# A hybrid decoder layer on one core: GpSimd in a fixed order while the attention patterns of one head pair are merged under the next

## The chip, the cores and the metric

The kernel runs on one core of one Trainium2 chip. The core has a matrix engine (TensorE, PE in the profile; PEld is its weight load), a vector engine (VectorE, DVE), a scalar engine (ScalarE, ACT), GpSimd (POOL) and SyncE (SP), which here issues only DMAs. Each engine works through a queue of its own in order, and a DMA is issued by an instruction in one of these queues. The metric is the time on the device of one execution, in microseconds (us).

## The reference

One layer of a causal decoder: a prompt of 2048 tokens and 64 sample tokens, width 1024. One projection feeds two mixers, a dilated softmax attention of 8 heads x 64 (mixer A) and a gated linear attention (mixer B); their outputs go side by side through the output projection `w_o`, and a convolutional feed-forward block follows. The change touches the prompt part of mixer A and the first chunk of the output projection.

```python
PATTERNS = ((128, 1), (512, 4), (2048, 16))       # (window, dilation)
def dilated_prompt(q, k, v, window, dil):
    ...                                           # query t reads keys t - j*dil, j = 0..window/dil
    s = jnp.einsum('brhcie,brhcje->brhcij', qb, kk) * (E ** -0.5)
    s = jnp.where(mask, s, NEG)
    lse = jax.nn.logsumexp(s, axis=-1)
    p = jnp.exp(s - lse[..., None])
    o = jnp.einsum('brhcij,brhcje->brhcie', p, vv)
    ...
    return o, lse
```

Every head is computed in three patterns. The three outputs of a head and position are then averaged with weights in proportion to their softmax denominators, exp(lse) of each over the sum of the three: this is the merge.

## The kernel before

**How the attention is cut.** `attention` (L986 on) works through four pairs of heads (`pr` 0 to 3; the two heads of a pair fill 128 columns). A pair has three patterns (`pat` 0 to 2, dilation 1, 4 and 16) of four groups `g`, twelve groups in all, counted here 0 to 11; the groups of patterns 0 and 1 are cut into two units each, those of pattern 2 are one unit, so there are 20 units per pair. For a unit, `AtUnit.qk_` issues the score matmuls (`pas`, L1787), a masked row minimum on VectorE (L1792) and the exponential on ScalarE (L1796). `drain` runs two and three units behind: the transposes of the probabilities (L1813, copied to `apt`), and the product with V into `pao` (L1830), of which VectorE copies the finished group to the block `aop` of that pattern (L63). `aop` has five buffers; a pair fills three, one for each pattern.

**Operands.** Patterns 1 and 2 read queries with a stride; GpSimd gathers them two groups ahead (`at_gather`, two copies `aqg` per group, L1118). SyncE loads Q and K of the next pair in pieces (`at_load`, L1073, a generator advanced once per group) and blocks of V (`at_loadv`, four DMAs each, L1085).

**The merge.** When the last unit of a pair is through, `at_merge` is made as a generator for that pair. Its first step aligns the three patterns' minima and sums by matmuls (`pam`), computes the three weights per head and position in small steps on [128 x 32] pieces (L1151 to L1166), transposes them, copies them to `awt` and stores them in DRAM (`d_awd`, L1184). A weight block is then loaded by GpSimd's queue as two DMAs, each a row of weights that all 64 partitions of a head receive (`awb`, two buffers, L1173). Four blocks `cb` follow: on GpSimd, three products of `aop` with the weights (L1211) and two sums (L1215, L1217) into `amo`, which is stored to `mixa` (L1219). `attention` advances the generator once per group of patterns 0 and 1 of the next pair. For pair 3 there is no next pair: its weights reach the columns through TensorE transposes (`pab`, L1208), the products are VectorE's (L1209), and its stores are on SyncE.

**What sets the order.** The Python order of the calls, as issued, gives a scheduler its program, and for GpSimd the scheduler may move instructions against each other; TensorE's attention instructions are chained in program order by `AtUnit.line`.

**Behind the attention.** `wo_pre` loads and splits the first operands of the output projection (`WORD`, four of mixer B, k = 4 to 7) during pair 3, `wo_x` the others: k = 0 to 3 are read back from `mixa`. A split makes the pieces `xh` and `xl` on ScalarE or VectorE (L71 is its subtraction). The matmuls are in `wo` (`pbo`, L1405).

## Time and profile before

| what | us |
|---|---|
| median of three timed runs | 2848.71 |
| lowest and highest of them | 2837.03, 2849.65 |
| the profiled execution, its own time | 2844.27 |
| the profiled execution, its span | 2842.5 |
| TensorE busy, whole span | 2682.9 (94%) |
| VectorE busy | 1841.9 (65%) |
| ScalarE busy | 1268.1 (45%) |
| GpSimd busy | 602.3 (21%) |

The profile is one execution as the hardware recorded it. Its page gives each engine's busy share, the span in 40 slices of 71 us with one digit per engine (tenths busy) and the TensorE clock that was granted, and groups of instructions. A row of a group or of the timeline reads: line and engine, operation, output <- inputs by the program's names (numbers cut off), shape, count; `[4.50 <-DMA d_mixa<-amo]` means that the engine was idle for 4.50 us before it and that this transfer ended the idle time. In a timeline the row begins with its start and its duration, in us. In the table of windows a row gives the start and end, the length, then for PE, PEld, DVE, ACT, POOL the busy time with the number of instructions, then the granted clock, the DMA share and GB/s.

### The profile page before, as it was taken

How to read it: one execution, taken by the hardware profiler on the slowest of the kernel's cores; microseconds unless marked ns; L12 is line 12 of the kernel's file. 1: busy time of each engine (PE TensorE's matmuls, PEld its weight loads, DVE VectorE, ACT ScalarE, POOL GpSimd, SP SyncE). 2: the span in 40 equal slices, each digit the busy share in tenths (PEclk: the TensorE clock that was granted, in tenths of full speed). 3: DMA queues.
4: the chain of work that ended last, by engine and by line, in shares of the span. 5: the costliest groups of instructions: out<-in, count | busy, mean ns of one | idle time of the engine just before them, and what ended most of it. 6: DMA issues, size and time to landing. Idle time of an engine off the chain costs nothing. (4 is left out here: it accounts for less than half of the span.)

```text
span 2842.5 us, 58662 instructions
## 1 busy us (share of the span) xinstructions
PE 2682.9 (94%) x22255; PEld 2529.1 (89%) x22255; DVE 1841.9 (65%) x4557; ACT 1268.1 (45%) x2958; POOL 602.3 (21%) x751
## 2 busy tenths in 40 slices
PE   7999999999988967998899999999999999999997
PEld 6788899788877856998899999899999999999997
DVE  7667654443356746466889988676567766666666
ACT  6535433333267855344455545443334433443332
POOL 3424242443324557003110002000020000200001
PEclk9999999999989989999999999999999999999998
DMA  8755445898888745267488668787588875876654
GB/s 296 256 176 183 166 146 180 299 329 328 288 176 172 180 113 126 92 207 284 173 284 297 234 224 306 277 289 265 199 313 285 294 264 190 323 256 216 221 191 146
DMA packets 285657, 657.09 MB, mean 231 GB/s; under 512 B 31856, under 2 KB 82672, under 8 KB 283328
## 3 DMA queue, kind: packets, MB, share of 16 engines
q1 hardware_dynamic: 254880, 576.50, 60.5%
q0 software_dynamic: 13408, 44.99, 5.1%
q10 hardware_dynamic: 17088, 31.86, 3.0%
q8 instruction: 175, 2.87, 0.4%
q14 instruction: 106, 0.87, 0.1%
HBM read 509.29 MB, written 143.94 MB: 230 GB/s over the span
## 5 line engine op out<-in xcount | busy, mean ns | idle before, releaser
L68 ACT ACTIVATE ws<-wr 128x512 fp32r<-128x512 f32 (+1 forms) x482 | 293.0, 616 | 434.3 <-PE pfe L1559 135.6
L90 PE MATMUL pfd<-hh,ws 128*128 128x264 f32 x2816 | 475.5, 285 | 8.7 <-ACT ws L68 4.4
L90 PEld LDWEIGHTS pfd<-hh,ws 128*128 128x128 f32 x2816 | 399.5, 188 | 11.9 <-ACT ws L68 5.8
L71 DVE TENSOR_TENSOR ws<-wr,ws 128x512 fp32r<-128x512 f32 (+1 forms) x482 | 319.4, 668 | 140.0 <-ACT ws L68 136.4
L90 PE MATMUL pfd<-hl,ws 128*128 128x264 f32 x1408 | 303.0, 284 | 1.2 <-DVE hl L71 1.2
L1559 PE MATMUL pfa<-xh,ws 128*128 128x264 f32 x1496 | 293.2, 287 | 5.5 <-ACT ws L68 3.2
L1559 PE MATMUL pfe<-xh,ws 128*128 128x264 f32 x1496 | 289.9, 286 | 4.0 <-DMA ws<-d_wst 2.5
L1559 PE MATMUL pfd<-xh,ws 128*128 128x264 f32 x1408 | 289.2, 285 | 0.3 <-DVE gt L1546 0.2
L1559 PEld LDWEIGHTS pfa<-xh,ws 128*128 128x128 f32 x1496 | 237.4, 190 | 7.5 <-ACT ws L68 3.9
L1559 PEld LDWEIGHTS pfe<-xh,ws 128*128 128x128 f32 x1496 | 237.4, 190 | 4.6 <-DMA ws<-d_wst 2.7
L396 PE MATMUL pv<-wh,xh 128*128 128x256 f32 (+1 forms) x816 | 234.2, 287 | 1.1 <-DVE th L693 1.1
L1559 PEld LDWEIGHTS pfd<-xh,ws 128*128 128x128 f32 x1408 | 231.9, 189 | 0.7 <-DVE gt L1546 0.4
L396 PE MATMUL pv<-wl,xh 128*128 128x256 f32 (+1 forms) x816 | 231.8, 284 | 0.0
L396 PE MATMUL pv<-wh,xl 128*128 128x256 f32 (+1 forms) x816 | 231.0, 283 | 0.0
L90 PEld LDWEIGHTS pfd<-hl,ws 128*128 128x128 f32 x1408 | 225.3, 188 | 1.6 <-DVE hl L71 1.6
L1796 ACT ACTIVATE ass<-ass,aml 128x256 f32<-128x256 f32 (+1 forms) x384 | 173.6, 454 | 112.4 <-DVE aml L1792 86.8
L1508 POOL DMA_DIRECT2D xl<-d_xst x52 | 28.6, 551 | 892.4 <-PE pfe L1559 856.5
L1559 PE MATMUL pfd<-xl,ws 128*128 128x264 f32 x704 | 200.9, 285 | 0.0
L90 PE MATMUL pq<-xh,wh 128*128 128x512 f32 (+2 forms) x480 | 174.4, 371 | 10.2 <-ACT xh L234 7.8
L1559 PE MATMUL pfa<-xl,ws 128*128 128x264 f32 x616 | 176.7, 287 | 0.7 <-DMA xl<-d_xst 0.7
L1559 PE MATMUL pfe<-xl,ws 128*128 128x264 f32 x616 | 175.2, 285 | 0.0
L90 PE MATMUL pq<-xl,wh 128*128 128x512 f32 (+2 forms) x480 | 173.7, 363 | 0.0
(335 smaller groups left out, 6609.4 us busy)
## 6 DMA issues: line engine op xcount, KB each, us to landing
ws<-d_wst SPq DMA_DIRECT2D x248, 512.0 KB
wr<-in_wu SPq DMA_DIRECT2D x114, 512.0 KB
d_wst<-ws SPq DMA_DIRECT2D x88, 512.0 KB
wr<-in_wd SPq DMA_DIRECT2D x160, 256.0 KB
wr<-in_wt SPq DMA_DIRECT2D x60, 512.0 KB
wh<-d_wbs SPq DMA_DIRECT2D x35, 512.0 KB
wl<-d_wbs SPq DMA_DIRECT2D x35, 512.0 KB
skp<-in_ckt SPq DMA_DIRECT2D x16, 1024.0 KB
```

Source lines behind the costliest of these rows:

```text
L68: h = nc.scalar.activation(hi, src, AF.Copy)
L71: return h, (nc.gpsimd if lo_eng == "p" else nc.vector).tensor_tensor(lo, src, hi.bitcast(F32), op=ALU.subtract)
L90: mm = nc.tensor.matmul(o, ww[:, k, :], xx[:, s0:s0 + n], start=(k == order[0] and i == 0), stop=(k == order[-1] and i == 2))
L396: mm = nc.tensor.matmul(ps[:m, :256], x[:, t0:t0 + m], w[:, k % 4, :], start=(k == 0 and i == 0), stop=(k == KT - 1 and i == 2))
L1508: self.nc.gpsimd.dma_start(t.bitcast(F32), xo[i, z])
L1559: self.lastmm = nc.tensor.matmul(bank[:, :H], w[:, ww, k, :], xx, start=new and k == 0 and j == 0, stop=k == 3 and j == 2, skip_group_chec ...
L1796: ex = nc.scalar.activation(ssb[:, sc:sc + nk], ssb[:, sc:sc + nk], AF.Exp, bias=self.ml[:, idx, h:h + 1], scale=-1.0, accum_out=self.ml[: ...
```

## The change

- A new `line` chains GpSimd's work of the attention in the order in which the program issues it: gathers, the store of the weights, their loads, products, sums and stores. The merge of pair 3 isn't chained, apart from its stores.
- The merge generator is advanced in every group of the next pair (before: groups 0 to 7), and a block takes two groups: products of patterns 0 and 1 and their sum (now into the block of pattern 1) in one, the product of pattern 2, the second sum and the store in the other. Two more stops lie around the store of the weights.
- The loads of the next pair's Q and K are advanced in groups 5 to 10 (before: 0 to 7).
- The small steps of the merge are VectorE's for pairs 0 to 2 and GpSimd's for pair 3 (before: the other way round).
- The weights lie in another order in DRAM, so that a block is read as one run of 1536 elements per partition (before: twelve runs of 128).
- `amo` has two buffers, and pair 3 takes `amo` from a ring of six (`ass`); `apt` has four buffers, not five; pair 3's stores are GpSimd's.
- The eight DMAs of the first two V blocks are issued by GpSimd, not by SyncE.
- `wo_pre` prepares three operands (k = 4, 5, 6), `wo_x` five (k = 7 and 0 to 3); the piece of k = 3 that chunk 0 needs is split straight from pair 3's `amo`, and not read back.

```diff
-    AB = dict(... pt=5 ... ms='ppps' ...)
+    AB = dict(... pt=4 ... ms='pppp' ...)
...
-            p.tile([128, 512], F32, name=self.n("amo"), tag="amo", bufs=1)
+            for _ in range(2):
+                p.tile([128, 512], F32, name=self.n("amo"), tag="amo", bufs=2)
...
-                        if pend is not None and pat < 2:
+                        if pend is not None:
                             next(pend, None)
-                        if pat < 2:
+                        if 5 <= 4 * pat + g < 11:
                             self.qk0 = next(nxt, self.qk0)
...
     def at_loadv(self, i):
-        nc = self.nc
+        nc, e = self.nc, self.nc.gpsimd if i < 2 else self.nc.sync
...
+    def line(self, ins):
+        if self.atpo is not None:
+            self.after(ins, self.atpo)
+        self.atpo = ins
+        return ins
...
-            self.nc.gpsimd.tensor_copy(t, src)
+            self.line(self.nc.gpsimd.tensor_copy(t, src))
...
-        em = nc.vector if pr == 3 or not AB["em"] else nc.gpsimd
+        em, line = (nc.gpsimd, lambda x: x) if pr == 3 else (nc.vector, self.line)
...
-                    nc.gpsimd.dma_start(W[64 * h:64 * h + 64],
-                                      bass.AP(tensor=wd.tensor, offset=wd.offset + 128 * h + 256 * cb,
-                                              ap=[[0, 64], [4096, 3], [1024, 4], [1, 128]]))
+                    line(nc.gpsimd.dma_start(W[64 * h:64 * h + 64],
+                                           bass.AP(tensor=wd.tensor, offset=wd.offset + 1536 * (2 * cb + h),
+                                                   ap=[[0, 64], [512, 3], [128, 4], [1, 128]])))
...
-            nc.gpsimd.dma_start(wd, wt)
+            yield
+            line(nc.gpsimd.dma_start(wd, wt))
+            yield
             nxt = weights(0)
...
             for i in range(3):
+                if i == 2 and not last:
+                    line(nc.gpsimd.tensor_tensor(OP[1][:, :, sl], OP[1][:, :, sl], OP[0][:, :, sl], op=ALU.add))
+                    yield
...
-                    (nc.gpsimd if j % 12 < AB["mp"] else nc.vector).tensor_tensor(
-                        OP[i][:, :, sl], OP[i][:, :, sl], W[:, i], op=ALU.mult)
+                    line(nc.gpsimd.tensor_tensor(OP[i][:, :, sl], OP[i][:, :, sl], W[:, i], op=ALU.mult))
...
-            e.tensor_tensor(OP[0][:, :, sl], OP[0][:, :, sl], OP[1][:, :, sl], op=ALU.add)
...
+            if last:
+                mo = self.aq[1].tile([128, 512], F32, name=self.n("amo"), tag="ass", bufs=AB["s"])
+            else:
+                mo = p.tile([128, 512], F32, name=self.n("amo"), tag="amo", bufs=2)
...
+            le(e.tensor_tensor(mo.rearrange("p (m r) -> p r m", r=4),
+                               OP[1][:, :, sl], OP[2][:, :, sl], op=ALU.add))
+            line(nc.gpsimd.dma_start(self.a["mixa"][:, pr, 512 * cb:512 * cb + 512], mo))
+            if last and cb < 2:
+                if cb == 0:
+                    self.xnext[3] = self.hl()
+                o, m = ((0, 512), (512, 2 * H - 512))[cb]
+                self.split(*(t[:, o:o + m] for t in self.xnext[3]), mo[:, :m], "v")
...
-        for k in self.WORD[:4]:
+        for k in self.WORD[:3]:
...
-        for k in self.WORD[0 if c else 4:]:
+        for k in self.WORD if c else self.WORD[3:7]:
```

What the change does to the order shows on three engines. The first place is GpSimd's queue in pair 1, where the merge of pair 0 begins. Of before, the rows from the store of the weights on (`awb` are weight blocks, `aop` the three patterns' outputs, `aqg` gathered queries; a number is the program's own):

```order
L1184 DMA d_awd_73<-awt_1767_10587 96x128
L1173 DMA awb_1768_10590<-d_awd_73 64x12x128 x2
L1173 DMA awb_1790_10691<-d_awd_73 64x12x128 x2
L1211 TENSOR_TENSOR aop_1519_9386<-aop_1519_9386,awb_1768_10590 128x4x128
L1211 TENSOR_TENSOR aop_1592_9725<-aop_1592_9725,awb_1768_10590 128x4x128
L1211 TENSOR_TENSOR aop_1676_10101<-aop_1676_10101,awb_1768_10590 128x4x128
L1211 TENSOR_TENSOR aop_1519_9386<-aop_1519_9386,awb_1790_10691 128x4x128
L1211 TENSOR_TENSOR aop_1592_9725<-aop_1592_9725,awb_1790_10691 128x4x128
L1211 TENSOR_TENSOR aop_1676_10101<-aop_1676_10101,awb_1790_10691 128x4x128
L1215 TENSOR_TENSOR aop_1519_9386<-aop_1519_9386,aop_1592_9725 128x4x128
L1118 COPY aqg_1820_10821<-aqs_1590_9721 128x512
L1118 COPY aqg_1842_10927<-aqs_1529_9444 128x512
```

And the same place of the changed kernel:

```order
L1195 DMA d_awd_73<-awt_1767_10585 96x128
L1126 COPY aqg_1789_10688<-aqs_1630_9901 128x512
L1126 COPY aqg_1790_10690<-aqs_1686_10160 128x512
L1183 DMA awb_1808_10778<-d_awd_73 64x1536 x2
L1126 COPY aqg_1812_10788<-aqs_1630_9901 128x512
L1126 COPY aqg_1813_10790<-aqs_1686_10160 128x512
L1183 DMA awb_1831_10878<-d_awd_73 64x1536 x2
L1225 TENSOR_TENSOR aop_1520_9387<-aop_1520_9387,awb_1808_10778 128x4x128
L1225 TENSOR_TENSOR aop_1589_9714<-aop_1589_9714,awb_1808_10778 128x4x128
L1210 TENSOR_TENSOR aop_1589_9714<-aop_1589_9714,aop_1520_9387 128x4x128
L1126 COPY aqg_1833_10889<-aqs_1630_9901 128x512
L1126 COPY aqg_1834_10891<-aqs_1686_10160 128x512
```

Before, both weight blocks are loaded and six products and a sum stand together ahead of the next gathers; now a pair of gathers stands between the store, the first load, the second load and the second half step, and the first sum follows its two products.

The second place is SyncE's queue at the start of the attention (`aqs`, `akh`, `akl` are pieces of Q and of the two parts of K, `av` blocks of V). Before:

```order
L1073 DMA aqs_1488_9209<-d_qh0_57 64x512
L1073 DMA akh_1494_9246<-d_kh0_65 64x512 x2
L1085 DMA av_1502_9349<-out_o_vp 128x1x128 x4
L1085 DMA av_1503_9354<-out_o_vp 128x1x128 x4
L1073 DMA akl_1497_9277<-d_kl0_69 64x512 x2
L1085 DMA av_1520_9387<-out_o_vp 128x1x128 x4
L1073 DMA aqs_1479_9116<-d_qh0_57 64x2x512
```

And now:

```order
L1074 DMA aqs_1488_9209<-d_qh0_57 64x512
L1074 DMA akh_1494_9246<-d_kh0_65 64x512 x2
L1074 DMA akl_1497_9277<-d_kl0_69 64x512 x2
L1086 DMA av_1521_9388<-out_o_vp 128x1x128 x4
L1074 DMA aqs_1479_9116<-d_qh0_57 64x2x512
```

The eight DMAs of two V blocks are gone from between `akh` and `akl`; they stand in GpSimd's queue.

The third place is VectorE's queue at the end of pair 3's merge and the start of the output projection (`pab` are transposed weights, `xl` is the second piece of a split operand, `br` a raw operand). Before:

```order
L1209 TENSOR_TENSOR aop_2369_13432<-aop_2369_13432,pab_2446_13872 128x4x128
L1215 TENSOR_TENSOR aop_2176_12575<-aop_2176_12575,aop_2269_13012 128x4x128
L1217 TENSOR_TENSOR amo_2438_13831<-aop_2176_12575,aop_2369_13432 128x4x128
L1217 TENSOR_TENSOR amo_2443_13857<-aop_2176_12575,aop_2369_13432 128x4x128
L71 TENSOR_TENSOR xl_2452_13899<-br_2453_13900,xh_2451_13898 128x528
L71 TENSOR_TENSOR xl_2455_13905<-br_2456_13906,xh_2454_13904 128x528
```

And now:

```order
L71 TENSOR_TENSOR xl_2431_13800<-amo_2429_13795,xh_2430_13799 128x512
L1233 TENSOR_TENSOR aop_2266_12993<-aop_2177_12576,aop_2266_12993 128x4x128
L1223 TENSOR_TENSOR aop_2266_12993<-aop_2266_12993,pab_2444_13865 128x4x128
L1223 TENSOR_TENSOR aop_2177_12576<-aop_2177_12576,pab_2443_13858 128x4x128
L71 TENSOR_TENSOR xl_2431_13800<-amo_2436_13825,xh_2430_13799 128x16
L1223 TENSOR_TENSOR aop_2364_13410<-aop_2364_13410,pab_2445_13872 128x4x128
L1235 TENSOR_TENSOR amo_2441_13853<-aop_2266_12993,aop_2364_13410 128x4x128
L1233 TENSOR_TENSOR aop_2266_12993<-aop_2177_12576,aop_2266_12993 128x4x128
L1235 TENSOR_TENSOR amo_2446_13879<-aop_2266_12993,aop_2364_13410 128x4x128
L1353 MEMSET halo_16438 128x44
L71 TENSOR_TENSOR xl_2452_13900<-br_2453_13901,xh_2451_13899 128x528
L71 TENSOR_TENSOR xl_2455_13906<-br_2456_13907,xh_2454_13905 128x528
```

Two splits straight from `amo` (512 and 16 columns) now stand among the merge's steps, the two last sums write to buffers of the larger ring, and the splits of the operands that are read from DRAM still come behind both sums.

More of the change, by code (lines that the diff above doesn't have):

```diff
@@ L1134, in at_merge @@
         else:
-            tm = p.tile([128, 512], F32, name=self.n("atm"), tag="amo", bufs=1)
+            tm = p.tile([128, 512], F32, name=self.n("atm"), tag="amo", bufs=2)
         nc.vector.tensor_tensor(tm[:, :256].rearrange("p (o b x) -> p o b x", o=16, b=4),
@@ L1180, in at_merge @@
             nc.tensor.transpose(pt[:96, :128], awf, self.ident)
-            wt = p.tile([128, 512], F32, name=self.n("awt"), tag="amo", bufs=1)[:96, :128]
+            wt = p.tile([128, 512], F32, name=self.n("awt"), tag="amo", bufs=2)[:96, :128]
             self.evac(wt, pt[:96, :128], "v")
             wd = self.a["awd"][pr]
-            nc.gpsimd.dma_start(wd, wt)
+            yield
+            line(nc.gpsimd.dma_start(wd, wt))
+            yield
             nxt = weights(0)
@@ L1195, in at_merge @@
                 W, nxt = nxt, weights(cb + 1) if cb < 3 else None
-            mo = p.tile([128, 512], F32, name=self.n("amo"), tag="amo", bufs=1)
             for i in range(3):
+                if i == 2 and not last:
+                    line(nc.gpsimd.tensor_tensor(OP[1][:, :, sl], OP[1][:, :, sl], OP[0][:, :, sl], op=ALU.add))
+                    yield
                 if last:
```

34 lines of the change are left out of this document (17 added, 17 removed).

## The prediction

> **What bounds the kernel now.** I read the page first: TensorE (PE) is busy nearly everywhere and falls at one place only, the slices from 780 to 1140 us, which are the prompt attention. Its granted clock falls there too.
>
> ```profile
> span 2842.5 us, 58662 instructions
> PE   7999999999988967998899999999999999999997
> PEclk9999999999989989999999999999999999999998
> ```
>
> The profiled execution took 2844.27 us, that is its span and 1.8 us around it; the three timed runs have a median of 2848.71, so the sum below, made against 2844.27, may lie 4 us below a median. Next I read TensorE's timeline for the first score matmul of each pair (one row per pair), and of three pattern-16 groups (842.69, 853.83 and 988.85).
>
> ```profile
> 779.83 0.22 PE L1787 MATMUL pas<-akh,aqs 128*128 128x128 f32 x1
> 842.69 0.33 PE L1787 MATMUL pas<-akh,aqg 128*128 128x128 f32 x1
> 853.83 0.33 PE L1787 MATMUL pas<-akh,aqg 128*128 128x128 f32 x1
> 857.69 0.33 PE L1787 MATMUL pas<-akh,aqs 128*128 128x128 f32 x1
> 939.78 0.33 PE L1787 MATMUL pas<-akh,aqs 128*128 128x128 f32 x1
> 988.85 0.33 PE L1787 MATMUL pas<-akh,aqg 128*128 128x128 f32 x1
> 1008.23 0.33 PE L1787 MATMUL pas<-akh,aqs 128*128 128x128 f32 x1
> 1103.24 0.33 PE L1787 MATMUL pas<-akh,aqg 128*128 128x128 f32 x1
> ```
>
> The pairs take 77.9, 82.1, 68.5 and, up to the last group at 1103.24, 95.0 us. Undisturbed they would take this: pair 2 needs 988.85 - 939.78 = 49.1 us for its first eight groups, in which nothing waits, and pair 0 needs 857.69 - 842.69 = 15.0 us for four groups of pattern 16, of which the last starts after 11.1. So an **undisturbed pair is 64.1 us**, its group 11 starting at 60.2. Who waits in 800 to 1160 us, from the view of waits on TensorE, its three longest lines:
>
> ```profile
> PE pao L1830 <- DVE aop L63: 22.8, 1, 22.8
> PE pas L1787 <- POOL aqg L1118: 21.8, 4, 10.7
> PE pbo L1405 <- DVE xl L71: 7.6, 1, 7.6
> ```
>
> Two of them are GpSimd (POOL). 21.8 us are gathers that stand behind a merge. The 22.8 us, in pair 3, are a VectorE (DVE) copy that waits until the merge of pair 1 has finished with its first block; the rows show that merge waiting for its weights and adding only at 1033:
>
> ```profile
> 1028.99 3.70 POOL L1211 TENSOR_TENSOR aop<-aop,awb 128x512 f32<-128x512 f32 x3 [3.19 <-DMA awb<-d_awd]
> 1033.27 2.49 POOL L1215 TENSOR_TENSOR aop<-aop,aop 128x512 f32<-128x512 f32 x2
> 1036.91 1.34 PE L1830 MATMUL pao<-apt,av 128*64 128x128 f32 x10 [22.78 <-DVE aop L63]
> 999.57 0.33 PE L1787 MATMUL pas<-akh,aqg 128*128 128x128 f32 x1 [2.33 <-POOL aqg L1118]
> ```
>
> The last row prices what follows a short wait: pair 2 took 68.45 us, 64.1 and 2.3 of waiting, so **2.0 us** went to the slower clock behind it.
>
> **Pairs 1 to 3: the new GpSimd order.** It has the same 16 gathers, 12 products and 8 additions per merge, but each merge is spread over eleven groups, and a gather now stands in a fixed place between half steps. I price that queue from these rows (products, gathers; then issues with KB each and median time to landing).
>
> ```profile
> L1118 POOL CAST aqg<-aqs 128x512 fp32r<-128x512 f32 x60 | 64.3, 1100 | 39.9 <-PE pas L1787 38.5 <-issue 1.5
> L1211 POOL TENSOR_TENSOR aop<-aop,awb 128x512 f32<-128x512 f32 x36 | 44.6, 1269 | 34.3 <-DMA awb<-d_awd 34.3
> L1173 POOL DMA_DIRECT2D awb<-d_awd x24 | 18.0, 756 | 9.8 <-DMA d_awd<-awt 8.0 <-issue 1.7
> awb<-d_awd POOLq DMA_DIRECT2D x24, 384.0 KB, 10.9
> d_mixa<-amo POOLq DMA_DIRECT2D x12, 256.0 KB, 3.8
> d_awd<-awt POOLq DMA_DIRECT2D x3, 48.0 KB, 4.3
> 876.37 0.56 POOL L1184 DMA_DIRECT2D d_awd<-awt  x1 [2.61 <-DVE awt L63]
> 884.26 2.99 POOL L1173 DMA_DIRECT2D awb<-d_awd  x4 [7.34 <-DMA d_awd<-awt]
> 897.10 7.36 POOL L1211 TENSOR_TENSOR aop<-aop,awb 128x512 f32<-128x512 f32 x6 [9.84 <-DMA awb<-d_awd]
> ```
>
> In pair 1 the weights are stored at 876.37, 18.7 us after the pair began. The copy ahead of the store now stands one unit (2.9 us) later in VectorE's order, so 21.6. Then come the store (0.6), its landing La, the issue of the first weight block (1.5), its landing Lw, and the first product starts at 23.7 + La + Lw. From there to the first gather of group 11 the fixed order holds three leading half steps (3 x 1.27 = 3.8 each), two trailing ones (2 x 1.27 and a store of 0.6: 3.1 each), two weight issues (1.5 each) and nine gathers (1.1 each): 11.4 + 6.2 + 3.0 + 9.9 = 30.5 us. The gather is then ready at 54.2 + La + Lw, and TensorE wants it at 60.2, so it comes **late by La + Lw - 6.0**. The groups of pattern 16 last 3.7 us, while two gathers and half a step take 6: that is why the wait gathers there.
>
> La: 7.3 us where the loads of the next pair's Q and K run beside it (the wait in the row at 884.26), 4.3 in the median; I take 5.5 for pairs 1 and 2 and 4.3 for pair 3, which loads no next pair. Lw is unknown, since no weight block is loaded in runs of 6 KB before. The upper bound is today's: 12.8 from issue (884.26) to first use (897.10), less the 1.5 of issuing, 11.3. The nearest row from below is the store of `mixa` from the same queue, 256 KB in unbroken rows, 3.8. A block is 768 KB; at the 222 GB/s of a busy stretch (row below) that is 3.5 us, and 2 for the rest: I take Lw = 5.5. Pairs 1 and 2 are late by 5.0, pair 3 by 3.8; with 2.0 for the clock that makes 64.1 + 7.0 = **71 us** for each of pairs 1 and 2 (gains of 11.1, and a loss of 2.5), and 60.2 + 5.8 = **66.0** for pair 3 up to its group 11, a gain of 29.0. Bounds: nothing late gives 64.1 and 60.2; Lw = 11.3 and La = 7.3 give 78.7 twice and, with La = 4.3, 71.8.
>
> The Trainium skill prices this load by itself: "DMA: Bandwidth & Descriptors", section "Anatomy of one DMA", fits 2.0 us and bytes / 436e3 for a DMA from GpSimd, so 3.8 us as an estimate for a block of 768 KB. The row of 10.9 us for half of it does not agree with that for today's loads; by that price the sum would be 5 us lower.
>
> The 22.8 us go with the same order: the block of the merged pair that the next copy needs is free after the last leading half step, 7 us behind the last gather, at about 72, and TensorE needs the copy for its third product of pattern 16, two units into the next pair, at about 76. The margin is 4 us; without it that much would come back.
>
> Beside other work, at nothing: the small merge steps, now on VectorE, are 12 of about 0.2 us per merge (row below), 2.4 us under pairs in which VectorE is busy for 50.6 of 68; uncovered they cost 7 in all. The transposed blocks fall from 5 to 4, but TensorE's fixed order finishes the product of unit n-4 before it transposes unit n-2; uncovered, that is a product of 1.0 us per unit. `amo` gets a second buffer, which only removes waits. In SyncE's order the next pair's loads keep their place behind the buffers they wait for; uncovered, a pair would start with the 1.8 us of waiting for a piece that the row at 805.57 below shows.
>
> ```profile
> L1155 DVE TENSOR_TENSOR aaw<-aw,amm 128x32 f32<-128x32 f32 x2 | 0.4, 188 | 0.0
> 940.00:1008.00 68.00, 65.47 (x657) 58.17 (x658) 50.56 (x231) 56.02 (x217) 32.97 (x42) 0.97 0.73 163
> ```
>
> **Pair 0.** SyncE issues eight loads of V ahead of a K piece that TensorE wants. They move to GpSimd's queue, so the pieces behind them are issued up to 7.5 us sooner.
>
> ```profile
> 777.47 7.51 SPq L1085 DMA_DIRECT2D av<-out_o_vp  x8
> 780.00:790.00 10.00, 4.91 (x28) 4.36 (x28) 4.32 (x24) 4.99 (x21) 0.54 (x1) 0.77 0.57 158
> 790.00:800.00 10.00, 5.03 (x36) 4.23 (x34) 3.17 (x15) 4.55 (x16) 1.09 (x1) 0.84 1.01 222
> 805.57 0.55 PE L1787 MATMUL pas<-akl,aqs 128*128 128x256 f32 x1 [1.75 <-DMA akl<-d_kl]
> ```
>
> But the same bytes must land before 805.57, and only the ten microseconds with a DMA share of 0.57 have room: 4.3 us at most, 0 at least. I take 2.9: pair 0 becomes **75.0**. The eight issues delay GpSimd's last store of V by about 4.5 us; its columns belong to pairs 2 and 3, and the first gather starts only at 794.
>
> **The end.** From the last group to the output projection it takes 1142.69 - 1103.24 = 39.45 us. TensorE waits there for operand pieces (`xl`) that VectorE writes behind the last two sums of pair 3:
>
> ```profile
> 1137.41 1.06 DVE L1217 TENSOR_TENSOR amo<-aop,aop 128x512 f32<-128x512 f32 x1 [4.50 <-DMA d_mixa<-amo]
> 1141.00 1.10 DVE L1217 TENSOR_TENSOR amo<-aop,aop 128x512 f32<-128x512 f32 x1 [2.53 <-DMA d_mixa<-amo]
> 1141.93 2.55 DVE L71 TENSOR_TENSOR xl<-br,xh 128x528 fp32r<-128x528 f32 x4
> 1142.69 0.81 PE L1405 MATMUL pbo<-xl,wh 128*128 128x264 f32 x2 [7.63 <-DVE xl L71]
> ```
>
> Both sums wait for a store out of the one `amo` buffer: 4.50 + 2.53 = 7.0 us. Pair 3 now takes its buffers from a ring of six, so these go. Added are two splits straight from the sums (a split is 2.55 / 4 = 0.6 at 528 columns; 512 and 16 columns make 0.8 together). One block of matmuls (k = 7) that ran under the wait now stands behind it: 0.7. That is 39.45 - 7.0 + 0.8 + 0.7 = **34.0**. Late next is VectorE itself, with its products of pair 3. Bounds: the whole 7.63 gone, or 3 if the splits and the block cost twice what I put down and the small steps of pair 3, now on GpSimd (12 at 246 ns and not at 188: +0.7), stand on the path.
>
> **Sum.** Before: 77.9 + 82.1 + 68.45 + 95.0 + 39.45 = 362.9. After: 75.0 + 71 + 71 + 66.0 + 34.0 = 317.0. The gain of 45.9 makes 2844.27 - 45.9 = **2798 us**.
>
> **Rivals.**
> *All is hidden.* The weights land as fast as the stores (3.8 us), the gathers of pattern 16 are in time, and the pairs take 64.1, 64.1 and 60.2: with 75.0 and 34.0 that is 297.4, so **2779**. For it: the row of 3.8 us from the same queue. Against it: the load is three times that store (768 KB a block), and the queue has only 60.2 - 54.2 = 6.0 us for La + Lw. Chance 0.18.
>
> *The loads are no faster.* Lw stays 11.3, La 7.3: 78.7, 78.7, 71.8, 75.0 and 34.0 make 338.2, so **2820**. For it: what fills the DMA engines in a merge is the same bytes in both kernels, and the share was 0.73 to 1.01 in the rows above. Against it: 768 KB in 11.3 us is 68 GB/s where other stretches reach 222. Chance 0.17. The Trainium skill speaks for this rival: "DMA: Bandwidth & Descriptors", section "Specifications", sets the smallest transfer for line rate at 512 B, which today's runs have already. The trace does not bear that out alone, as the 384 KB of 512 B runs take 10.9 us against 3.8 for 256 KB in rows; which of size and run length does it, no row says.
>
> *Slower: the gathers are held behind the weights.* In the fixed order a late block stops every gather behind it, and TensorE with them, where today a scheduler's order put gathers as they came. The price is La + Lw - 6.0 in each of three merges. It eats the whole gain when the three pairs lose another 45.9 / 3 = 15.3 each, that is from La + Lw = 26.3 on, against 11.0 in my sum. The slowest landing of half a block is below:
>
> ```profile
> DMA to landing us min/median/max: 7.0/10.9/16.6
> ```
>
> 16.6 + 7.3 = 23.9, still under 26.3. A merge of eleven groups must also be done before its `aop` blocks are wanted again, and the margin of 4 us above could fall with it; both together give about 2860. Chance 0.04.
>
> *No change.* The order doesn't do what it says: the groups of pattern 16 wait as long in sum as the two longest waits of TensorE now, 22.8 + 21.8 = 44.6, and only the clock and the end move: 2830 to 2858. Chance 0.08.
>
> **How the numbers follow.** Forecast 2798 with 0.53, the rivals 0.18, 0.17, 0.04 and 0.08. Half a per cent, 14 us, is about what a measurement of this kernel can tell from no change. The forecast and the first two rivals are all faster by more: 0.88; the same 0.08, slower 0.04. The range goes from the first rival less 5 (pair 0 at 73.6 and the end at 31.8 would be 3.6 less), 2774, to the second plus 4 (pair 0 at 77.9, the end 1 us longer), 2824; it leaves out the last two rivals.
>
> **What would show it.** Right: no wait of TensorE for the copy of `aop` (22.8 now); its waits for `aqg` in short pieces in groups 8 to 11 of pairs 1 to 3, 3 to 6 us a pair, with `awb` as what GpSimd waits for; `awb` landing in 4 to 7 us; the first score rows of the pairs some 75, 71 and 71 us apart; sums of pair 3 without a wait for `d_mixa`. The second rival shows in a median landing of `awb` near 11, the first in no wait for `aqg` at all. Pair 0 is wrong if the first wait for `akl` stays. The forecast fails if a new long wait stands on TensorE: for `apt`, of which there are four, for a piece of Q or K at a pair's start, or for weights stuck behind the V loads on GpSimd's queue.

## The result and the profile after

The changed kernel takes 2799.83 us (median of four runs, 2796.51 to 2802.07), the kernel before 2849.18 (2837.03 to 2849.88): a ratio of **0.9836, 95% interval 0.9808 to 0.9864**. The profiled execution took 2799.56 us, 44.7 less than the one before. In the page TensorE's share rises with its busy time unchanged, and the five slices of the attention stand at 8, 9, 9, 9 and 8 tenths (8, 8, 9, 6 and 7 before):

```profile
span 2797.8 us, 58627 instructions
PE 2685.3 (96%) x22255; PEld 2532.2 (91%) x22255; DVE 1844.2 (66%) x4580; ACT 1268.5 (45%) x2959; POOL 595.0 (21%) x741
PE   7999999999989998998999998999999999999997
PEclk9999999999999999998999999999999999999998
```

TensorE's timeline, first score matmul of each pair and of the last group (line 1809 now):

```profile
781.37 0.22 PE L1809 MATMUL pas<-akh,aqs 128*128 128x128 f32 x1
855.13 0.33 PE L1809 MATMUL pas<-akh,aqs 128*128 128x128 f32 x1
931.24 0.33 PE L1809 MATMUL pas<-akh,aqs 128*128 128x128 f32 x1
1008.70 0.33 PE L1809 MATMUL pas<-akh,aqs 128*128 128x128 f32 x1
1074.05 0.33 PE L1809 MATMUL pas<-akh,aqg 128*128 128x128 f32 x1 [2.78 <-POOL aqg L1126]
```

The landmark of the end, the matmul that waited for `xl`, has no wait any more. I use the last matmul of the output projection in its place, from the view by line; its last start stands ahead of the semicolon. Before:

```profile
L1405 PE MATMUL pbo<-xh,wl x512: 279/284/422, 1132.2 to 1336.6; 128*128 128x264 f32 x171
```

And after:

```profile
L1427 PE MATMUL pbo<-xh,wl x512: 278/284/423, 1100.6 to 1297.0; 128*128 128x264 f32 x171
```

So the 44.7 us go where this table says (the end: last group to last output matmul, 1336.6 - 1103.24 = 233.4 before and 1297.0 - 1074.05 = 222.9 after):

| stretch | before | after | change | forecast |
|---|---|---|---|---|
| pair 0 | 77.9 | 73.8 | -4.1 | -2.9 |
| pair 1 | 82.1 | 76.1 | -6.0 | -11.1 |
| pair 2 | 68.5 | 77.5 | +9.0 | +2.5 |
| pair 3 to its last group | 95.0 | 65.4 | -29.7 | -29.0 |
| the end | 233.4 | 222.9 | -10.4 | -5.5 |
| all before and behind these | | | -3.6 | 0 |

The last line I don't put down to the change, which touches nothing there: what follows the output projection took 1497.0 to 1507.3 us in the profiles of the fourteen kernels here, and 1505.9 and 1500.8 in these two. Without it, -41.2 was measured where -45.9 was forecast. The end varies too, from 220.7 to 226.9 us in the ten kernels here whose operations at the end are the changed kernel's.

The large waits of before (22.8 for the copy of `aop`, 21.8 for gathers) are gone. Of TensorE's waits from 780 to 1110 us these are the three longest; the first was forecast by no step:

```profile
PE pao L1852 <- DMA av<-out_o_vp: 10.4, 4, 3.9
PE pas L1809 <- POOL aqg L1126: 6.8, 5, 2.8
PE pas L1809 <- DMA akh<-d_kh: 4.0, 1, 4.0
```

The forecast priced pairs 1 to 3 by one quantity, the sum La + Lw of two landings. GpSimd's timeline gives it: the store of the weights, then the first product of the merge, less 0.5 for the store and 1.5 for the issue. First pair 1, then pair 2, then pair 3:

```profile
877.54 0.53 POOL L1195 DMA_DIRECT2D d_awd<-awt  x1 [27.72 <-PE pao L1852]
895.24 2.48 POOL L1225 TENSOR_TENSOR aop<-aop,awb 128x512 f32<-128x512 f32 x2 [8.54 <-DMA awb<-d_awd]
954.51 0.54 POOL L1195 DMA_DIRECT2D d_awd<-awt  x1 [15.29 <-DVE awt L63]
973.13 2.52 POOL L1225 TENSOR_TENSOR aop<-aop,awb 128x512 f32<-128x512 f32 x2 [4.78 <-DMA awb<-d_awd]
1031.73 0.53 POOL L1195 DMA_DIRECT2D d_awd<-awt  x1 [14.52 <-DVE awt L63]
1042.73 2.98 POOL L1225 TENSOR_TENSOR aop<-aop,awb 128x512 f32<-128x512 f32 x2 [2.11 <-DMA awb<-d_awd]
```

895.24 - 877.54 - 2.0 = 15.7, and likewise 16.6 and 9.0, where 11.0, 11.0 and 9.8 were put down. The first issue of weights lies between the two (pairs 1, 2 and 3):

```profile
882.50 1.05 POOL L1183 DMA_DIRECT2D awb<-d_awd  x2 [2.21 <-DMA d_awd<-awt]
962.81 1.04 POOL L1183 DMA_DIRECT2D awb<-d_awd  x2 [5.57 <-DMA d_awd<-awt]
1034.44 1.04 POOL L1183 DMA_DIRECT2D awb<-d_awd  x2
```

From its end to the first product it is 11.7, 9.3 and 7.2 us, where Lw was 5.5; from the end of the store to the issue it is 4.4, 7.8 and at most 2.2, where La was 5.5, 5.5 and 4.3. (Gathers run under both; in pairs 2 and 3 one of them waits for TensorE, and the product still waits for the weights behind it.) Into the forecast's own rule (late by La + Lw - 6.0, 2.0 for the clock) the sums give 75.8, 76.7 and 65.2 us; measured were 76.1, 77.5 and 65.4. That made the question for the experiments: is it this landing that sets the pairs, or V, for which TensorE waits by the list, and what makes the landing long?

Times below are medians of device time. The changed kernel's four runs span 2796.5 to 2802.1, so a few us can't be told from 2800 by times alone; the stretches of the trace can be read finer. The kernel before, timed again beside each group of runs, has medians from 2844.7 to 2849.2.

### The profile page after: what moved, and what is told of

The parts are those of the page before. It is cut to its first block, busy times and chain, and to the rows that moved or that the text cites. A ratio compares the mean times of both kernels' runs of the same rounds, so it can differ in the third digit from the quotient of the medians.

```text
span 2797.8 us, 58627 instructions
## 1 busy us (share of the span) xinstructions
PE 2685.3 (96%) x22255; PEld 2532.2 (91%) x22255; DVE 1844.2 (66%) x4580; ACT 1268.5 (45%) x2959; POOL 595.0 (21%) x741
## 4 chain that ended last, share of the span: by engine, by line
PE 76%; DMA 9%; DVE 7%; POOL 3%; ACT 2%; issue 2%; SPq 1%; ACTq 0%; DVEq 0%; POOLq 0%
PE pfd L90 17%; PE pv L396 9%; PE pfe L1581 8%; PE pfa L1581 8%; PE pfd L1581 8%; PE pq L90 7%; PE pbo L1427 5%; PE pfb L1581 4%; PE pas L1809 2%; PE pao L1852 1%; DMA ws<-d_wst 1%; PE pat L1835 1%; DMA raw<-in_xp 1%; DVE ws L71 1%; POOL aop L1225 1%
## 5 line engine op out<-in xcount | busy, mean ns | idle before, releaser
L90 PEld LDWEIGHTS pfd<-hh,ws 128*128 128x128 f32 x2816 | 401.7, 189 | 10.9 <-ACT ws L68 5.3
L90 PEld LDWEIGHTS pfd<-hl,ws 128*128 128x128 f32 x1408 | 226.9, 189 | 1.7 <-DVE hl L71 1.7
L1609 DVE TENSOR_TENSOR acc<-acc,pfd 128x264 f32<-128x264 f32 x304 | 116.9, 427 | 91.3 <-PE pfd L90 91.0
```

What stands on the lines that cost most here:

```text
L90: mm = nc.tensor.matmul(o, ww[:, k, :], xx[:, s0:s0 + n], start=(k == order[0] and i == 0), stop=(k == order[-1] and i == 2))
L1609: nc.vector.tensor_tensor(acc[m][:, s0:s0 + n], acc[m][:, s0:s0 + n], pz, op=ALU.add)
```

## The experiments

### The two halves of the new order

**No chain.** GpSimd's queue is left to the scheduler again; steps, groups and loads stay as changed.

```diff
     def line(self, ins):
-        if self.atpo is not None:
-            self.after(ins, self.atpo)
-        self.atpo = ins
         return ins
```

> The changed kernel without the chain on GpSimd: the half steps, the groups and the loads stay, but the scheduler is free to order GpSimd's queue. If the fixed order carries the gain of pairs 1 to 3 (45 us of it), gathers stand behind whole blocks again: long waits of TensorE for gathered queries, 2825 to 2845 us. If the half steps over eleven groups do it by themselves, the time stays within 5 us of 2800.

2812.03 us (2808.83 to 2814.61; ratio 0.9867, interval 0.9843 to 0.9891), between the two expectations. Pairs 1 to 3 take 85.2, 72.9 and 73.8 us, 12.9 more in sum than with the chain, and the waits of before come back in small (from TensorE's waits, 780 to 1110 us):

```profile
PE pas L1806 <- POOL aqg L1123: 20.0, 7, 8.0
PE pao L1849 <- DVE aop L63: 6.8, 2, 4.9
```

So the chain is worth some 12 us, about half of the 26.7 us by which pairs 1 to 3 are shorter than before (245.6 then, 218.9 now), and not the gain.

**Whole steps.** The chain stays, but a block's second half is no longer put off to the next group.

```diff
                 if i == 2 and not last:
                     line(nc.gpsimd.tensor_tensor(OP[1][:, :, sl], OP[1][:, :, sl], OP[0][:, :, sl], op=ALU.add))
-                    yield
```

> The half steps undone: a block (three products, two sums, store) stands whole between the gathers of two groups, in the same fixed order; merges then end by group 7 of the next pair. Theory (queue): the gathers of groups 6 and 7 stand behind whole blocks and a first load of 16 us: a pair waits 6 to 10 us more there than with half steps but catches up behind group 8: pairs 1 to 3 lose 0 to 8 us each, 2805 to 2820 us. Rival: the half steps are worth most of what the fixed order is not, some 30 us: 2830 us.

2846.74 us; against the kernel before a ratio of 1.0007 (0.9989 to 1.0026): **the whole gain is gone**, more than either theory said. The first product comes as early as ever (40.3 us after the start of pair 1), but TensorE waits at every block. Its timeline in pair 1:

```profile
905.97 0.47 PE L1808 MATMUL pas<-akh,aqg 128*128 128x128 f32 x1 [5.28 <-POOL aqg L1126]
916.39 0.33 PE L1808 MATMUL pas<-akh,aqg 128*128 128x128 f32 x1 [1.79 <-POOL aqg L1126]
926.74 0.47 PE L1808 MATMUL pas<-akh,aqg 128*128 128x128 f32 x1 [6.55 <-POOL aqg L1126]
936.03 0.48 PE L1808 MATMUL pas<-akh,aqg 128*128 128x128 f32 x1 [2.83 <-POOL aqg L1126]
```

The idle times sum to 16.5 us in this pair, and the pair takes 89.8 us. Pair 0 and the end keep their gains in this run (73.9 and 224.4 us), so pairs 1 to 3, at 257.2 us in sum, are even worse than before the change (245.6), and some 38 us worse than with half steps. The half steps make the fixed order work. I had expected the lost time to be caught up behind the merge; the rows show why it isn't: each wait is followed by the next block.

### Is it V or the weights?

**No Q and K.** Left out: the loads of Q and K for pairs 2 and 3, which compute with pair 1's.

```diff
-                nxt = self.at_load(pr + 1) if pr < 3 else iter(())
+                nxt = self.at_load(pr + 1) if pr < 1 else iter(())
```

> Left out: the loads of Q and K for pairs 2 and 3 (these pairs compute with pair 1's), 6.3 MB less in the windows of pairs 1 and 2 each. Theory (weights): pairs 1 and 2 (76.1 and 77.5 us now) are long because the first weight block lands late beside these loads; store and block then take 9 to 10 us in sum as in pair 3, and a pair takes 64.1 + 3.5 + 2 = 69 to 70 us: 2784 to 2788 us, with short waits for gathers left and none for V. Rival (V): what sets the pairs is V arriving late; no wait is left and a pair takes 64 to 66: 2774 to 2780 us.

Pairs 1 and 2 take 69.0 and 71.2 us, about as the theory of the weights says (69 to 70); 2793.54 us (2789.23 to 2799.12), 5.5 above its range. First products come 33.4 and 34.3 us after their pair's start, La + Lw is 9.0 and 8.9, and what waits is the gathers:

```profile
PE pas L1809 <- POOL aqg L1126: 9.3, 6, 2.8
```

The run takes traffic from beside V as well: it shows that the weights still hold the pairs when V is in time, not that V held nothing.

**No V.** Left out: the loads of V for pairs 1 to 3, which compute with pair 0's last block.

```diff
     def at_loadv(self, i):
+        if i >= 12:
+            self.vq += self.vq[-4:]
+            return
```

> Left out: the loads of V for pairs 1 to 3 (they compute with pair 0's last block), so no product can wait for V. Theory (weights): the waits for V (10.4 us) turn into waits for gathers, since these were due at the same time; pairs 1 and 2 keep 70 to 77 us, less only by what the first weight block lands sooner: 2788 to 2800 us. Rival (V): the waits for V go and nothing takes their place, pairs 1 and 2 take 64 to 67 us: 2774 to 2782 us.

2780.99 us (2776.43 to 2782.2), by its time what the rival says. But the trace shows pairs 1 and 2 at 71.5 and 66.1, with gathers waited for, as the theory says, and with La + Lw at 10.0 and 6.7. By time this run spoke for V, by its parts for the weights: taking V away also takes traffic from beside the weights, so it can't tell the two apart. That is done by three runs made for other ends (below), whose code in pair 1 is the changed kernel's, and whose loads differ only in pair 0 or at the end. TensorE's waits in pair 1, of the changed kernel:

```profile
PE pao L1852 <- DMA av<-out_o_vp: 7.0, 3, 3.9
```

Of the run in which `mixa` is read back:

```profile
PE pas L1804 <- POOL aqg L1126: 8.4, 4, 3.7
```

And of that with the first V loads on SyncE (in the third, with one buffer at the end, it is 6.4 us for gathers and none for V):

```profile
PE pas L1809 <- POOL aqg L1126: 8.8, 4, 4.2
```

In one execution TensorE waits for V and never for a gather, in three others for gathers and never for V, and the pair takes 76.1 us in the first and 79.0, 79.4 and 76.1 in these: both come at about the same time, the list names the one that was a little later, and without a wait for V the pair is no shorter. The run with the small steps on GpSimd (below) shows the other side: there the first product of pair 1 comes 2.8 us sooner than in the changed kernel, TensorE waits for V alone, and the pair still takes 75.7 us:

```profile
PE pao L1852 <- DMA av<-out_o_vp: 7.3, 3, 5.4
```

So either of the two, left alone, holds pair 1 at about 76 us. What the runs with this order of GpSimd share is a rule, counted not from La + Lw but from the pair's start, so that it also takes pairs whose store is late: a pair lasts as long as its first product takes to come, and 36.4 us more (30.5 of queue, 3.9 for the last group, 2.0 for the clock); pair 3 to its last group, 32.5 more. The queue came out as forecast: from the first product to the end of the last gather, one gather more than in the 30.5, pair 1 shows 30.7 to 31.8 us in the ten kernels that keep this order. A part of their thirty pairs:

| run, pair | first product after | by the rule | measured |
|---|---|---|---|
| changed, 1 | 40.1 | 76.5 | 76.1 |
| changed, 2 | 41.9 | 78.3 | 77.5 |
| changed, 3 | 34.0 | 66.5 | 65.4 |
| no Q and K, 1 | 33.4 | 69.8 | 69.0 |
| no V, 2 | 31.9 | 68.3 | 66.1 |
| short runs, 2 | 42.5 | 78.9 | 80.0 |
| V on SyncE, 1 | 42.8 | 79.2 | 79.4 |
| Q and K later, 2 | 46.2 | 82.6 | 83.2 |
| small steps on GpSimd, 1 | 37.4 | 73.8 | 75.7 |

The rule misses by 2.2 us at most. In the last row, 1.9 over it, V holds the pair: its last gather was done 7.5 us before the pair's end, in pair 1 of the others 4.3 to 6.1.

### What makes the landing long?

**Short runs.** The weights lie in DRAM as before the change, and a block is read in runs of 512 bytes.

```diff
-        at = lambda i: cap(aw, 4 * i, [[1, 4], [24, 4], [12, 2]])
+        at = lambda i: cap(aw, 32 * i, [[8, 4], [2, 4], [1, 2]])
...
-                                           bass.AP(tensor=wd.tensor, offset=wd.offset + 1536 * (2 * cb + h),
-                                                   ap=[[0, 64], [512, 3], [128, 4], [1, 128]])))
+                                           bass.AP(tensor=wd.tensor, offset=wd.offset + 128 * h + 256 * cb,
+                                                   ap=[[0, 64], [4096, 3], [1024, 4], [1, 128]])))
...
-                    src = cap(aw, 24 * cb + 4 * i, [[1, 4], [12, 2], [0, 64]])
+                    src = cap(aw, i * 32 + 2 * cb, [[8, 4], [1, 2], [0, 64]])
```

> The weights lie as before the change, so a block is loaded in runs of 512 bytes and not of 6 KB. Theory: the run length is worth what the first block's landing shows; it took 11.7, 9.3 and 7.3 us from issue to product in pairs 1 to 3 and would take 11.3 to 12.8 again, so pair 1 stays, pairs 2 and 3 lose 2 and 4 us: 2804 to 2808 us. Rival: run length is worth nothing, the traffic beside it sets the landing: 2800 +- 2 us.

2816.55 us (2807.57 to 2816.83; ratio 0.9879, 0.9855 to 0.9902): slower than both said. In the profiled execution, the fastest of the four, pairs 1 to 3 take 76.7, 80.0 and 69.6, 7.4 more than in the changed kernel, most of it in pair 3. What the other three, at 2816.4 to 2816.8, spend 9 us more on, no trace shows. The landing of half a block (minimum, median, maximum) of the changed kernel:

```profile
DMA to landing us min/median/max: 4.4/7.9/12.1
```

And of short runs:

```profile
DMA to landing us min/median/max: 6.0/9.2/15.8
```

Run length is worth 1.3 us at the median, traffic more: without Q and K the median is 5.5, without V 5.1. So the rival, run length worth nothing, falls, but it is the smaller part of the landing.

**Q and K later.** The same bytes; SyncE's loads stand in a fixed order from pair 1 on, the next pair's first head behind V's eighth block, its second behind the tenth.

```diff
-                        if 5 <= 4 * pat + g < 11:
+                        for _ in range((0, 0, 0, 0, 0, 3, 0, 3, 0, 0, 0, 0)[4 * pat + g]):
                             self.qk0 = next(nxt, self.qk0)
...
+                        if pr > 1:
+                            self.sline(ld)
...
+            if i > 13:
+                self.sline(ld)
```

> New: SyncE's loads from pair 1 on stand in a fixed order, with the next pair's Q and K not ahead of V's fifth block but behind the eighth (first head) and the tenth (second head). The same bytes in all; but the first weight block is no longer loaded beside Q and K. Theory (the traffic beside it sets the landing): store and first block land in 9 to 11 us in sum, not 16, and pairs 1 and 2 take 69 to 72 us: 2786 to 2792 us. Rival (the bytes must land anyway): the wait moves to the start of the next pair, to a piece of Q or K: 2797 to 2805 us.

2812.63 us (2808.67 to 2818.21): slower than the rival's range too, and right for both in part. Pair 1 takes 69.95 us with La + Lw at 9.1, as the theory says: with every byte of V still loaded and Q and K alone moved out of the way; the only wait left in it is 3.1 us for gathers. But pairs 2 and 3 pay at their start, and what comes late there puts off the whole merge. TensorE at the start of pair 2:

```profile
927.56 0.45 PE L1820 MATMUL pas<-akh,aqs 128*128 128x128 f32 x1 [3.79 <-DMA akh<-d_kh]
932.57 0.45 PE L1820 MATMUL pas<-akl,aqs 128*128 128x128 f32 x1 [4.56 <-DMA akl<-d_kl]
```

**Q and K between.** The second head one V block earlier.

```diff
-                        for _ in range((0, 0, 0, 0, 0, 3, 0, 3, 0, 0, 0, 0)[4 * pat + g]):
+                        for _ in range((0, 0, 0, 0, 0, 3, 3, 0, 0, 0, 0, 0)[4 * pat + g]):
```

> The run before with the second head's Q and K one V block earlier, behind the ninth and not the tenth V block (in its trace these pieces were issued 11 us before the pair that wants them, and that pair waited 8.4 us). Theory (the first weight block wants its few us without Q and K beside it, and these want to be issued in time): pair 1 keeps 70 to 72 us, and pairs 2 and 3 lose their waits at the start: 70 to 73 and 64 to 67 us, 2786 to 2791 us. Rival (in any order the bytes push something late): 3 to 8 us of waiting stay at the start of pairs 2 and 3, or V comes late: 2796 to 2806 us.

2813.06 us (2805.53 to 2817.73), the rival and more: pairs 1 to 3 take 70.1, 81.9 and 77.9. Now V is late in pair 2 and a piece of K in pair 3 (TensorE's waits from 780 to 1100 us; of the 9.3 for K, 5.0 are pair 0's and 4.3 pair 3's):

```profile
PE pas L1820 <- DMA akl<-d_kl: 9.3, 4, 4.3
PE pas L1820 <- DMA av<-out_o_vp: 7.3, 2, 4.2
```

Why no order of the loads tried is better than the changed kernel's, the windows of its pairs 1 to 3 suggest (start and end, length, busy time of five engines, then the clock, the **DMA share** and GB/s):

```profile
855.13:931.24 76.11, 69.07 (x662) 60.88 (x660) 51.59 (x243) 55.62 (x218) 41.55 (x43) 0.93 0.85 182
931.24:1008.70 77.46, 70.28 (x661) 61.49 (x659) 52.01 (x242) 57.54 (x224) 48.69 (x49) 0.93 0.82 188
1008.70:1074.05 65.35, 60.72 (x621) 53.44 (x619) 53.21 (x229) 54.49 (x204) 45.40 (x46) 1.00 0.64 163
```

0.85 x 76.1 = 65 us of a pair's DMA engines are busy, and 0.82 x 77.5 = 64: as long as an undisturbed pair of TensorE (64.1). In pair 2 before, of which I took the undisturbed pair, the share was 0.73 of 68 us, 50 us; two of the four weight blocks of that merge were issued only in pair 3 (at 1008.52 and 1013.42). That the bytes bound pairs 1 and 2 in any order isn't shown by this; only these orders were tried, and Q and K in groups 0 to 7, as before the change, were not.

### The other parts

**One buffer.** Pair 3's four sums go to one buffer.

```diff
-                mo = self.aq[1].tile([128, 512], F32, name=self.n("amo"), tag="ass", bufs=AB["s"])
+                mo = mo if cb else self.aq[1].tile([128, 512], F32, name=self.n("amo"), tag="ass", bufs=AB["s"])
```

> The changed kernel, with the four sums of pair 3 written to one and the same buffer, as before the change; the straight splits and all else stay. Theory: two waits of VectorE for stores come back, 4.5 and 2.5 us, ahead of the splits of the operands that TensorE waits for: the stretch from the last group to the end of the output projection (223.0 us) becomes 228 to 230, 2805 to 2808 us. Rival: the straight splits give TensorE enough to do and the end doesn't move: 2800 us.

2806.71 us (2803.75 to 2808.79), and the end takes 231.7 us where the changed kernel takes 222.9. The waits are back in VectorE's queue, and TensorE's with them (6.20 us for `xl`, at 1111.50):

```profile
1105.35 1.10 DVE L1235 TENSOR_TENSOR amo<-aop,aop 128x512 f32<-128x512 f32 x1 [1.39 <-DMA d_mixa<-amo]
1109.79 1.07 DVE L1235 TENSOR_TENSOR amo<-aop,aop 128x512 f32<-128x512 f32 x1 [3.34 <-DMA d_mixa<-amo]
```

In the changed kernel the same two sums follow without an idle time:

```profile
1100.49 1.11 DVE L1235 TENSOR_TENSOR amo<-aop,aop 128x512 f32<-128x512 f32 x1
1102.16 1.10 DVE L1235 TENSOR_TENSOR amo<-aop,aop 128x512 f32<-128x512 f32 x1
```

**Read back.** The straight splits undone, four operands prepared ahead (`WORD[:4]`), k = 3 of chunk 0 read from `mixa`.

```diff
-            if last and cb < 2:
-                if cb == 0:
-                    self.xnext[3] = self.hl()
-                o, m = ((0, 512), (512, 2 * H - 512))[cb]
-                self.split(*(t[:, o:o + m] for t in self.xnext[3]), mo[:, :m], "v")
...
-        for k in self.WORD[:3]:
+        for k in self.WORD[:4]:
...
-        for k in self.WORD if c else self.WORD[3:7]:
+        for k in self.WORD[0 if c else 4:]:
```

> The straight splits undone: k = 3 of chunk 0 is read back from mixa and four operands are prepared ahead, as before the change; the ring of buffers stays. Theory: the gain at the end came from the ring, so the stretch from the last group to the end of the output projection stays within 2 us of 223.0: 2798 to 2802 us. Rival: reading the last piece back makes TensorE wait for store and load behind the last sum, 5 to 6 us: 2805 us.

2799.13 us (2797.67 to 2802.2), the end 221.3: the theory. With the ring of buffers in place, the straight splits are worth nothing that can be measured.

**V on SyncE.** The first eight V loads back in SyncE's queue (`e = self.nc.sync` for every block).

> The eight loads of the first two V blocks back on SyncE. Theory: pair 0 goes from 73.8 back to 76 to 78 us, nothing else moves: 2802 to 2804 us. Rival: pair 0 is bound by the bytes that must land and its gain came from something else in the change: 73 to 75 us, 2800 us.

2802.73 us (2801.35 to 2806.98). The times touch the changed kernel's, but pair 0 takes 77.8 us, and 73.4 to 75.6 in the twelve other profiles that have these loads on GpSimd: some 4 us, as the theory says.

**Small steps on GpSimd** for pairs 0 to 2, on VectorE for pair 3.

```diff
-        em, line = (nc.gpsimd, lambda x: x) if pr == 3 else (nc.vector, self.line)
+        em, line = (nc.vector, lambda x: x) if pr == 3 else (nc.gpsimd, self.line)
```

> The small steps of the merge back on GpSimd for pairs 0 to 2 and on VectorE for pair 3. Theory: they stand ahead of the store of the weights, at 0.25 us each and with waits between the engines, so the first product comes 1 to 3 us later in pairs 1 to 3, and nothing else moves: 2801 to 2808 us. Rival: VectorE is relieved and nothing waits for the small steps: 2797 to 2800 us.

2801.35 us (2796.99 to 2811.5), pairs 1 to 3 at 75.7, 75.2 and 66.3: no difference that this can tell, but not for a reason that either expectation gave. On GpSimd the small steps bring the store sooner, 18.7, 18.8 and 20.9 us after the pair's start (22.4, 23.3 and 23.0 in the changed kernel), and the first product 2.8, 0.9 and 0.8 us sooner, where the theory had it later. In pair 1 TensorE then waits for V instead.

**Trailing half on VectorE.** An attempt at a faster kernel: the third product and second sum of pairs 0 to 2 are VectorE's, and the store is issued one group later.

```diff
-                    line(nc.gpsimd.tensor_tensor(OP[i][:, :, sl], OP[i][:, :, sl], W[:, i], op=ALU.mult))
+                    (nc.vector.tensor_tensor if i == 2 else lambda *x, **k: line(nc.gpsimd.tensor_tensor(*x, **k)))(OP[i][:, :, sl], OP[i][:, :, sl], W[:, i], op=ALU.mult)
...
+            if not last:
+                e, le = nc.vector, lambda x: x
             le(e.tensor_tensor(mo.rearrange("p (m r) -> p r m", r=4),
                                OP[1][:, :, sl], OP[2][:, :, sl], op=ALU.add))
-            line(nc.gpsimd.dma_start(self.a["mixa"][:, pr, 512 * cb:512 * cb + 512], mo))
+            if last or cb == 3:
+                line(nc.gpsimd.dma_start(self.a["mixa"][:, pr, 512 * cb:512 * cb + 512], mo))
...
                 yield
+                if not last:
+                    line(nc.gpsimd.dma_start(self.a["mixa"][:, pr, 512 * cb:512 * cb + 512], mo))
```

> New: for pairs 0 to 2 the trailing half step (third product, second sum) goes to VectorE, and GpSimd issues the store one group later. GpSimd's queue between the first product and the gather of group 11 is shorter by 2 x 2.55 us. Theory (weights and queue set the pairs): pairs 1 and 2 go from 76 and 77.5 to 71 and 72.5 us, pair 3 from 65.4 to 62: 2786 to 2790 us. Rival (V sets pairs 1 and 2): these keep 75 to 77 us with longer waits for V, pair 3 alone gains: 2796 to 2798 us. Rival 2: VectorE, 52 us busy of 76, becomes the bound with 5.4 us more: 2800 us or over.

2803.18 us (2799.73 to 2808.61): the second rival by its time, but not for the reason that it gave. The gathers are in time (waits of 0.8 us at most), yet now the product on VectorE waits for the weights with the row minima of the scores queued behind it. First VectorE's waits in pair 1:

```profile
DVE aop L1225 <- DMA awb<-d_awd: 12.2, 2, 9.2
```

And TensorE's timeline, at the first of these:

```profile
900.60 0.58 PE L1814 MATMUL pas<-akh,aqg 128*128 128x256 f32 x1 [6.34 <-DVE aml L1819]
```

The same late block is waited for in another queue, one in which TensorE has more at stake; VectorE was busy for only 54 us of 74.

## Why the prediction came out

The time, 2799.83 for a forecast of 2798, is better than its terms: that it fits to 2 us is in part luck, as the last lines of this section add up.

- **Bound and order: right.** Both long waits named are gone. The margin of 4 us for the copy of `aop` held: no wait for it was left.
- **The rule for pairs 1 to 3 (late by La + Lw - 6.0): right** where the store comes about as early as forecast, to 1 us in the changed kernel's three pairs. Where it comes late the rule must count from the first product (pair 2 of "Q and K later" takes 83.2 us, where La + Lw of 9.2 would give 69.3); so put, it holds to 2.2 us in the ten kernels that keep the new queue on GpSimd. The split between waiting and clock came out otherwise: pair 1 is 12.0 us over 64.1, of which 7.0 are waits, at a clock of 0.93 and with TensorE busy for 69.1 us (65.5 in pair 2 before), where the forecast put 2.0 on the clock. What the runs added is that the half steps carry the gain: without them the whole gain goes, without the chain some 12 us.
- **La and Lw: mis-sized.** The forecast's "I take Lw = 5.5" and La = 5.5 for pairs 1 and 2 came out as 15.7 and 16.6 in sum; pair 3 at 9.0 for 9.8. In pair 1 the load alone took 11.7, just over the upper bound of 11.3 that the forecast had from the kernel before; in pair 2 it took 9.3, and the store's landing 7.8. The second rival (78.7 each) is the nearer one there, and of the forecast's signs the landing of `awb` in 4 to 7 us failed (7.9 at the median). I weighed the bound by bytes and rate without the Q, K and V that land beside it: with Q and K held back the sum for the same bytes is 9.1. The two pairs cost 11.6 us more than forecast.
- The Trainium skill's price for this load ("DMA: Bandwidth & Descriptors", section "Anatomy of one DMA"), an estimate of 3.8 us for a block of 768 KB, isn't borne out here: half a block took 3.9 us at the least, in the runs without V and with whole steps, and 7.9 at the median in the changed kernel. Of its 512 bytes for line rate (section "Specifications") the short runs show that longer pieces still helped, by 1.3 us of landing.
- **A wait for V: not foreseen.** 10.4 us of it stand in the list, but with it gone in pair 1 (three runs) the pair was no shorter. It hides the wait for gathers in the changed kernel. But it is a second limit at the same place, which the forecast did not have: with the first product 2.8 us sooner (small steps on GpSimd), V held pair 1 at 75.7.
- **Pair 0: right** in that the loads moved to GpSimd do it, 4.1 us for 2.9 (V on SyncE: 77.8 again). But by the forecast's own sign, that the first wait for `akl` goes, it is wrong: 2.7 us of it stay at 787.29 (1.0 and 2.0 by 788.45 before). What is gone are the later ones, 1.89 (0.23 is left) and 1.75 for `akl` and 2.24 for `akh`.
- **The end: mis-sized.** -10.4 where 5.5 was forecast and 7.6 was the bound. The ring alone is worth 8.8 in the trace (231.7 against 222.9) and 6.9 by time. The wait of 7.63 is wholly gone; the rest lies ahead of the projection, whose first matmul starts 28.5 us after the last group before (at 1131.77) and 25.9 now (at 1099.95). Why isn't shown; before, GpSimd's two sums of pair 3 waited 1.89 and 2.31 us for a store out of the one buffer too. Whether the 0.8 for the splits and the 0.7 for the block of k = 7 are there can't be told: the run that reads back is 1.6 shorter at the end, less than the end varies.
- **Costed at nothing: right** as far as waits go: TensorE waits 1.0 us for `apt` in pairs 2 and 3, and for nothing of the small steps or the second buffer. That the small steps delay the store on VectorE was in the forecast (21.6 us, and 22.4 to 23.3 came).

The pairs' error (+11.6, less 1.9 in pairs 0 and 3) and the end's (-5.0) cancel in part, and 3.6 us came from stretches that the change doesn't touch. Without this luck the terms were 4.7 us short (-41.2 for -45.9).

## To carry to other kernels

Where one engine serves both a critical consumer and a long background job, cut the job into pieces that fit between two services before fixing the order: here pairs 1 to 3 took 11.6 us more than before with the order and whole pieces, 13.7 less with half pieces and no order, and 26.7 less with both. Price a load by what lands beside it in the changed schedule, not by its own bytes, and take an undisturbed stretch only from one that carried the traffic it will carry. And where two inputs come due together, a list of waits names one of them by chance: take each away, or compare executions, before calling it the cause.

## Not expected of the hardware

The same bytes of half a block landed in 3.9 to 16.6 us over these runs, with the traffic beside them: medians 5.1 (no V), 5.5 (no Q and K), 7.9 (changed), and in runs of 512 bytes 9.2 (short runs) and 10.9 (before). And with the same instructions in pair 1, one execution waits for V and three for gathers, at 76.1 to 79.4 us.
